# An MLP's seven-product schemes: one PSUM bank for each product, or products chained in shared banks

## The chip, the cores and the metric

The kernel runs on one core of one Trainium2 chip. Its time is the device time of one execution in microseconds (us); for a set of runs the median is given. The core has a matrix engine (PE; its weight loads are shown apart as PEld), three engines for elementwise work (DVE, ACT, POOL), and queues that issue transfers (SP's above all). Matmul results land in PSUM, eight banks of 512 fp32 columns in each of 128 partitions. In this kernel PE, DVE and ACT touch PSUM, and POOL works only in SBUF.

## The reference, cut to what matters

One layer of a flow-matching backbone on 640 tokens (128 of a prompt, 512 of a sample), width 1024: a mixer block, then an MLP with a squared ReLU. The edit touches the MLP alone:

```python
def _ffn_sub(x, shift, scale, gate, w_pre, w_post, w1, w2):
    h = _rms(x, w_pre) * (1 + scale) + shift
    f = jnp.square(jax.nn.relu(h @ w1)) @ w2
    return x + gate * _rms(f, w_post)
```

`w1` is 1024 x 4096 and `w2` 4096 x 1024. All is fp32.

## The kernel before, in words

**Precision.** Every fp32 operand is split into a rounded high part and a remainder (`split`, L165: ACT casts `whi`, then DVE, or POOL where `eng=G`, subtracts to get `wlo`). A product is three matmuls: high x high, high x low, low x high.

**Groups.** The 4096 hidden columns are worked in eight groups of 512, g = 0 to 7. A group has a first product (`ff1`, hidden values from `h` and `w1`), the squared ReLU, and a second product (`ff2`, its share of the output from the hidden values and `w2`). Group 0's first product (`ff1_first`, L1147) is made in the plain way, and so is group 7's second product, after the loop. All others use a scheme that makes a 2 x 2 block product from seven block products instead of eight, with sums of blocks before and after.

**ff1(g), g = 1 to 7 (L1165).** The weight block is cut into A11, A21, A22, A12 and the activations into B11 to B22 (two halves of the width, and the tokens in 64-column halves). POOL makes the weight sums S1 = A21 + A22, S2 = S1 - A11, S3 = A11 - A21, then S2' = A12 - S2, in tiles of `sm` (L1135). Each of the seven products runs in two halves of 12 matmuls with 320 columns, each half in a bank of its own; `ps_ff` (L1143) hands out five banks in turn (two `ps_mm`, three `ps_st`). DVE adds each finished half to a sum in SBUF, in `add` (L1189, recorded at L1191): 7 x 2 = 14 adds, and ACT copies the first product (L1196). `done` (L1186) is the squared ReLU in place, on DVE, four times.

**fops(c) (L1224)** makes ff2's left operands from ff1's four tiles `c11` to `c22`, again sums of blocks on POOL (L1237 to L1243) and splits on ACT and DVE (L1216, L1217).

**ff2(g - 1) (L1256).** The right operands are sums T1, T2, T3, T2' of blocks of `w2`, on POOL. Each of the seven products runs in two halves of 6 matmuls with 512 columns, and each half goes to one of three banks in turn (`ps_t3`, L121: two `ps_tp`, one `ps_tb`). The prompt's tokens have two plain products of 12 matmuls (`prompt`). `collect` (L1250) adds each bank to a running sum in SBUF, on DVE (L1254); for g = 0 it is a copy by ACT (L1252). There are eight such sums, `R[0]` to `R[7]`: one for each product and one for the prompt. What the scheme adds up from its seven products is put off to the end: seven POOL additions of whole sums after the loop (L1326).

**Loop (L1307).** For g = 1 to 7: `ff1(g)`, then `ff2(g - 1)`, then `fops` for g. After it group 7's second product is made, added to the sums (L1347), normalised and stored.

**Order of the work.** The program is built with `schedule_with_timeline_sim=True` (L1445): a planner of the framework orders each engine's instructions from its own estimate of durations, with the written order as priority. So the order in the trace isn't always the written one; PE, for instance, begins the next ff1 between two halves of ff2's last product. Each engine then works through its list in order. Weight loads are issued by SP's queue in order, into five buffers (L1037); a load waits until its buffer's former block has been read for the last time.

Of the kernel before, what the change touches and what calls it, by code (L numbers as in the profile page):

```python
# [18 lines left out]
P = 128  # L19
# [77 lines left out]
def body(ctx: ExitStack, tc: tile.TileContext, I, O, dbg=None):  # L97
# [1037 lines left out]
    def sm(name, a=None, b=None, op=None):  # L1135
        x = fa.tile([P, 1024], F32, tag="sm", name=name, bufs=2)
        if a is not None:
            G.tensor_tensor(x, a, b, op=op)  # L1138
        return x

    ffi = [1]

    def ps_ff():  # L1143
        ffi[0] = (ffi[0] + 1) % 5
        return ps_mm() if ffi[0] < 2 else ps_st(ffi[0] - 2)

    def ff1_first():  # L1147
        c = f_tiles()
        w = {q: load_w(I["w_ff1"][0, i], 4, 256) for q, i in (((0, 0), 0), ((1, 0), 3), ((0, 1), 1), ((1, 1), 2))}
        for t0, t1 in TG:  # L1150
            for fb in range(4):
                wd = (t1 - t0) * 128
                fs = slice(fb % 2 * 128, fb % 2 * 128 + 128)
                ps = ps_ff()
                mm3(by_tile(ps[:, :wd]), [(w[kh, fb // 2][0][:, k, fs], w[kh, fb // 2][1][:, k, fs],
                                           mhi[:, t0:t1, 4 * kh + k], mlo[:, t0:t1, 4 * kh + k])
                                          for kh in range(2) for k in range(4)])
                rl = sm("rl")
                S.activation(rl[:, :wd], ps[:, :wd], AF.Relu)
                for th in range(2):  # L1160
                    r = rl[:, :wd].rearrange("p (t h c) -> p t h c", h=2, c=64)[:, :, th]
                    V.tensor_tensor(c[fb // 2, th][:, fb % 2].rearrange("p (t c) -> p t c", c=64)[:, t0:t1], r, r, op=ALU.mult)
        return c

    def ff1(g):  # L1165
        A11, A21, A22, A12 = [load_raw(I["w_ff1"][g, i]) for i in range(4)]
        c = f_tiles()
        c11, u2, u3, c22 = c[0, 0], c[0, 1], c[1, 0], c[1, 1]

        def prod(raw, B):  # L1170

            hi, lo = split(raw, 4, 256)
            res = []
            for s in range(2):
                fs = slice(s * 128, s * 128 + 128)
                ps = ps_ff()[:, :320]
                for k in range(4):
                    bh, bl = [x[:, k] if len(x.shape) == 3 else x[:, :, k] for x in B]
                    o = ps if len(bh.shape) == 2 else ps.rearrange("p (t c) -> p t c", c=64)
                    PE.matmul(o, hi[:, k, fs], bh, start=(k == 0), stop=False)  # L1180
                    PE.matmul(o, hi[:, k, fs], bl, start=False, stop=False)  # L1181
                    PE.matmul(o, lo[:, k, fs], bh, start=False, stop=(k == 3))  # L1182
                res.append(ps)
            return res

        def done(x):  # L1186
            V.scalar_tensor_tensor(x, x, 0.0, x, op0=ALU.max, op1=ALU.mult)

        def add(out, a, b):  # L1189
            for s in range(2):  # L1190
                V.tensor_tensor(out[:, s], a[:, s], b[s], op=ALU.add)  # L1191

        B11, B12, B21, B22 = [[quad(x, *q) for x in (mhi, mlo)] for q in ((0, 0), (0, 1), (1, 0), (1, 1))]
        p = prod(A11, B11)
        for s in range(2):
            S.copy(u2[:, s], p[s])  # L1196
# [12 lines left out]
        done(u3)  # L1209
        G.tensor_tensor(S2, A12, S2, op=ALU.subtract)  # L1210
        add(u2, u2, prod(S2, B22))
        done(u2)
# [43 lines left out]
    def ff2(g, f):  # L1256
        B11, B21, B12, B22 = [w2_raw(g, *q) for q in ((0, 0), (1, 0), (0, 1), (1, 1))]

        def prod(i, name, w):
            for pair in range(2):  # L1260
                ps = ps_t3()
                mm3(ps, [(f[name][0][:, k, pair * 128 : pair * 128 + 128], f[name][1][:, k, pair * 128 : pair * 128 + 128],
                          w[0][:, k], w[1][:, k]) for k in range(2)])
                collect(R[i][:, pair], ps, g == 0)

        def prompt(n, w0, w1):
            ps = ps_t3()
            mm3(ps, [(f["pr"][0][:, 2 * i + k], f["pr"][1][:, 2 * i + k], w[0][:, k], w[1][:, k])
                     for i, w in enumerate((w0, w1)) for k in range(2)])
            collect(R[7][:, n], ps, g == 0)  # L1270
# [54 lines left out]
    for o, a, b in ((1, 0, 1), (5, 0, 5), (6, 5, 6), (2, 5, 2), (2, 2, 4), (3, 6, 3), (4, 6, 4)):  # L1325
        G.tensor_tensor(R[o], R[a], R[b], op=ALU.add)  # L1326
    with tc.tile_pool(name="fin", bufs=2, side="right", reuse_waits="tile") as fin_:
        gB2 = gate_bcast(1, fin_)
        w = {(kh, nh): split(w2_raw(7, kh, nh), 2, 512) for nh in range(2) for kh in range(2)}
        for blk in (None, (0, 0), (1, 0), (0, 1), (1, 1)):  # L1330
            r = 0 if blk is None else 1
            if blk is None:
                parts = [(slice(0, 128), 0, slice(0, 128))]
                y = [R[7][:, n] for n in range(2)]
                lhs = [[x[:, k] for x in fpr] for k in range(4)]
            else:
                th, pair = blk
                parts = [(slice(64 * j, 64 * j + 64), 1 + 2 * pair + j, slice(64 * th, 64 * th + 64)) for j in range(2)]
                y = [R[1 + 2 * th + n][:, pair] for n in range(2)]
# [119 lines left out]
```

## Time and profile before

| what | value |
|---|---|
| median of 3 runs | 1231.33 us (1230.71 to 1232.45) |
| profiled execution, its own time | 1229.95 us |
| its span, first to last instruction | 1228.0 us |
| mean granted clock of PE | 0.973 |
| loop over g | about 809 to 1196 us |

How to read the rows. A row of the timeline has the start (us), the duration (us), the engine, the source line, the operation, output <- inputs by the program's names, and, in brackets, how long the engine stood idle before it and what ended that. A row of groups has line, engine, operation, output <- inputs, shapes, xcount, then busy time and the mean ns of one, then the idle time before them. A row of stretches has start:end, length, then busy time (and instructions) of PE, PEld, DVE, ACT and POOL, PE's granted clock, the DMA share and GB/s. A row of waits has the waiting engine and line, the releaser, then us in total, times, and the longest. Matmul durations overlap, so the distance between starts is what counts.

### The profile page before, as it was taken

The numbers are of one execution on the slowest core, as the hardware profiler recorded it, in microseconds if no ns is written. First come the engines' busy times: TensorE is split into PE (matmuls) and PEld (weight loads), VectorE is DVE, ScalarE is ACT, GpSimd is POOL, SyncE is SP. The second block draws the span as 40 slices with busy tenths as digits, with TensorE's granted clock in tenths as the row PEclk, the third lists the DMA queues.
The fourth block names the chain that finished last, engine by engine and source line by source line (L and its number), as shares of the span: only waits on it lengthen the run. The fifth ranks groups of instructions, "written<-read, shape, count | busy, mean of one in ns | idle before, by whom it ended". The sixth has DMA issues, their size and how long they took to land. (4 is left out here: it accounts for less than half of the span.)

```text
span 1228.0 us, 24856 instructions
## 1 busy us (share of the span) xinstructions
PE 1123.9 (92%) x10111; PEld 986.2 (80%) x10111; DVE 947.3 (77%) x1689; ACT 478.0 (39%) x910; POOL 494.6 (40%) x322
## 2 busy tenths in 40 slices
PE   5999799898989799988999999989899989898896
PEld 3789799787777688887777899978878879796875
DVE  6568996675677666635756567899999999999996
ACT  5433344252423233224436253445443434344322
POOL 1442416150542110312311406656464556556555
PEclk9999999898989999989999999999999999999999
DMA  9721024444425433645334471021213223121405
GB/s 332 270 95 53 1 93 139 137 129 154 147 68 182 146 110 96 206 152 181 110 103 148 152 275 69 18 87 52 86 52 103 69 69 107 66 86 52 159 31 137
DMA packets 61313, 144.87 MB, mean 118 GB/s; under 512 B 12384, under 2 KB 26000, under 8 KB 61200
## 3 DMA queue, kind: packets, MB, share of 16 engines
q1 hardware_dynamic: 38528, 108.66, 26.2%
q10 hardware_dynamic: 22672, 34.64, 9.0%
q8 instruction: 79, 1.29, 0.4%
q14 instruction: 34, 0.28, 0.1%
HBM read 122.02 MB, written 21.25 MB: 117 GB/s over the span
## 5 line engine op out<-in xcount | busy, mean ns | idle before, releaser
L190 PE MATMUL ps_mm<-hhi,whi 128*128 128x320 f32 x576 | 185.8, 323 | 2.1 <-DVE gbn L244 1.5
L191 PE MATMUL ps_mm<-hlo,whi 128*128 128x320 f32 x576 | 183.1, 318 | 0.0
L192 PE MATMUL ps_mm<-hhi,wlo 128*128 128x320 f32 x576 | 182.8, 317 | 0.1
L171 DVE TENSOR_TENSOR wlo<-raw,whi 128x1024 fp32r<-128x1024 f32 x94 | 153.9, 1647 | 33.7 <-ACT whi L170 33.2
L170 ACT CAST whi<-raw 128x1024 fp32r<-128x1024 f32 x117 | 121.5, 1047 | 114.1 <-PE ps_tp L192 25.4
L190 PEld LDWEIGHTS ps_mm<-hhi,whi 128*128 128x128 f32 x576 | 111.4, 193 | 7.4 <-DVE gbn L244 1.9
L192 PEld LDWEIGHTS ps_mm<-hhi,wlo 128*128 128x128 f32 x576 | 111.4, 193 | 0.6
L191 PEld LDWEIGHTS ps_mm<-hlo,whi 128*128 128x128 f32 x576 | 111.4, 193 | 0.5
L171 POOL TENSOR_TENSOR wlo<-raw,whi 128x1024 fp32r<-128x1024 f32 x23 | 56.7, 2469 | 82.7 <-ACT whi L170 82.4
L1138 POOL TENSOR_TENSOR T<-raw 128x1024 f32<-128x1024 f32 x14 | 37.7, 2692 | 67.9 <-DVE wlo L171 32.6
L171 DVE TENSOR_TENSOR wlo<-T,whi 128x1024 fp32r<-128x1024 f32 x28 | 54.2, 1940 | 0.7 <-ACT whi L170 0.6
L170 ACT CAST whi<-T 128x1024 fp32r<-128x1024 f32 x28 | 29.4, 1053 | 64.0 <-PE ps_st L1181 19.6
L972 POOL TENSOR_SCALAR bias<-bias 128x256 f32<-128x256 f32 x24 | 25.2, 1057 | 70.6 <-DMA bias<-in_bias_dram 70.6
L480 DVE SCALAR_TENSOR_TENSOR y<-cvb,cw,y 128x644 f32<-128x644 f32 x48 | 49.2, 1026 | 0.7
L567 POOL TENSOR_TENSOR W<-cst,ghi 128x512 fp32r<-128x512 f32 x15 | 19.0, 1265 | 71.3 <-PE ps_tp L568 69.2
L1138 POOL TENSOR_TENSOR S<-raw 128x1024 f32<-128x1024 f32 x14 | 34.2, 2441 | 33.5 <-DVE wlo L171 33.5
L1254 DVE TENSOR_TENSOR R<-R,ps_tp 128x512 f32<-128x512 f32 x64 | 42.6, 676 | 2.6 <-PE ps_tp L192 2.3
L1182 PE MATMUL ps_st<-mhi,wlo 128*128 128x320 f32 x128 | 39.2, 309 | 0.3 <-DVE wlo L171 0.3
L1181 PE MATMUL ps_st<-mlo,whi 128*128 128x320 f32 x128 | 39.4, 308 | 0.0
L1180 PE MATMUL ps_st<-mhi,whi 128*128 128x320 f32 x128 | 39.3, 309 | 0.0
L170 ACT CAST whi<-S 128x1024 fp32r<-128x1024 f32 x28 | 29.2, 1047 | 24.8 <-POOL S L1138 24.8
L651 DVE TENSOR_TENSOR tq<-tq,Ud 128x16 f32<-128x16 f32 (+14 forms) x75 | 36.7, 489 | 1.9
(594 smaller groups left out, 3544.8 us busy)
## 6 DMA issues: line engine op xcount, KB each, us to landing
raw<-in_w_ff_dram SPq DMA_DIRECT2D x64, 512.0 KB
raw<-in_w_ada_dram SPq DMA_DIRECT2D x48, 512.0 KB
raw<-in_w_gate_dram SPq DMA_DIRECT2D x16, 512.0 KB
raw<-in_w_dn_dram SPq DMA_DIRECT2D x12, 512.0 KB
gt_d<-gth SPq DMA_DIRECT2D x32, 160.0 KB
gl<-gt_d ACTq DMA_DIRECT2D x16, 320.0 KB
raw<-in_w_qk_dram SPq DMA_DIRECT2D x8, 512.0 KB
raw<-in_w_br_dram SPq DMA_DIRECT2D x8, 512.0 KB
```

The costliest lines, as they stand in the source:

```text
L170: S.copy(hi, raw)
L171: eng.tensor_tensor(lo, raw, hi.bitcast(F32), op=ALU.subtract)
L190: PE.matmul(out, ah, bh, start=(i == 0), stop=False)
L191: PE.matmul(out, ah, bl, start=False, stop=False)
L192: PE.matmul(out, al, bh, start=False, stop=(i == n - 1))
L480: V.scalar_tensor_tensor(y, b[:, j : j + 644], cw[:, mt * 5 + j : mt * 5 + j + 1], y, op0=ALU.mult, op1=ALU.add)
L651: V.tensor_tensor(tq[:, q:, :], tq[:, q:, :], Ud[:, :, q].unsqueeze(1).to_broadcast([P, w, 16]), op=ALU.mult)
L1138: G.tensor_tensor(x, a, b, op=op)
L1180: PE.matmul(o, hi[:, k, fs], bh, start=(k == 0), stop=False)
L1181: PE.matmul(o, hi[:, k, fs], bl, start=False, stop=False)
L1182: PE.matmul(o, lo[:, k, fs], bh, start=False, stop=(k == 3))
L1254: V.tensor_tensor(dst, dst, ps, op=ALU.add)
```

## The change

In both schemes products that a result needs together are now chained in the same PSUM banks: later products add to what is there (`start` is not set for them), and the partial sum is read between two products.

- **ff1** has two bank pairs, `x` (the two `ps_mm`) and `y` (two `ps_st`). On `x` run A11 B11, then S2, S1 and S2' on top of it; on `y` runs A12 B21, and, taken anew, S3 and A22 on top. After A11 B11, S2 and S1, ACT copies the partial sum of `x` into a tile (`so_far`, six copies of half a pair instead of two); DVE adds `y` to a tile three times (six adds of 320 columns instead of 14). The fourth result is read from `x` by two ReLUs and a Square on ACT; the other three squared ReLUs stay on DVE.
- **ff2** chains A11, S2, S1 and S4 on `x` (two `ps_tp`), A12 on a pair `ps_tb` and `ps_st(2)`, and S3 and A22 on the same pair, taken anew. `prompt` uses `ps_tb`. `collect` is called as often as before, but into four sums and one for the prompt. In the first call (g = 0) six of the collects are DVE adds instead of ACT copies, since two products now go into one sum. The order is A11, A12, prompt, S2, S3, S1, A22, S4, prompt instead of A11, A12, prompt, S1, S2, A22, S3, S4, prompt.
- The seven POOL additions after the loop and the tile `R2` are gone, and `sm` has four buffers instead of two. `ff1_first` takes four banks in turn instead of five.

```diff
-        x = fa.tile([P, 1024], F32, tag="sm", name=name, bufs=2)
+        x = fa.tile([P, 1024], F32, tag="sm", name=name, bufs=4)
...
-    def ps_ff():
-        ffi[0] = (ffi[0] + 1) % 5
-        return ps_mm() if ffi[0] < 2 else ps_st(ffi[0] - 2)
+    def ps_ff(i):
+        return ps_mm() if i < 2 else ps_st(i - 2)
...
+        x = [ps_ff(s)[:, :320] for s in range(2)]
+
+        def prod(raw, B, ps, first=True, last=False):
...
+                    PE.matmul(o, hi[:, k, fs], bh, start=(first and k == 0), stop=False, skip_group_check=not first)
...
+        def so_far(out, ps):
             for s in range(2):
-                V.tensor_tensor(out[:, s], a[:, s], b[s], op=ALU.add)
...
-        p = prod(A11, B11)
-        for s in range(2):
-            S.copy(u2[:, s], p[s])
-        add(c11, u2, prod(A12, B21))
-        done(c11)
+                S.copy(out[:, s], ps[s])
+
+        def add(out, ps):
+            for s in range(2):
+                V.tensor_tensor(out[:, s], out[:, s], ps[s], op=ALU.add)
...
+        prod(A11, B11, x)
+        so_far(c[0, 0], x)
+        y = [ps_ff(2 + s)[:, :320] for s in range(2)]
+        prod(A12, B21, y, last=True)
+        add(c[0, 0], y)
+        done(c[0, 0])
         S1 = sm("S1", A21, A22, ALU.add)
         S2 = sm("S2", S1, A11, ALU.subtract)
-        add(u2, u2, prod(S2, TT[1]))
-        p = prod(S1, TT[0])
+        prod(S2, TT[1], x, False)
+        so_far(c[1, 0], x)
         S3 = sm("S3", A11, A21, ALU.subtract)
-        add(u3, u2, prod(S3, TT[2]))
-        add(u2, u2, p)
-        add(c22, u3, p)
-        done(c22)
-        add(u3, u3, prod(A22, B12))
-        done(u3)
+        y = [ps_ff(2 + s)[:, :320] for s in range(2)]
+        prod(S3, TT[2], y)
+        prod(S1, TT[0], x, False)
+        so_far(c[1, 1], x)
+        add(c[1, 1], y)
+        done(c[1, 1])
         G.tensor_tensor(S2, A12, S2, op=ALU.subtract)
-        add(u2, u2, prod(S2, B22))
-        done(u2)
+        prod(S2, B22, x, False, True)
+        for s in range(2):
+            S.activation(c[0, 1][:, s], x[s], AF.Relu)
+        S.activation(c[0, 1], c[0, 1], AF.Square)
+        prod(A22, B12, y, False, True)
+        add(c[1, 0], y)
+        done(c[1, 0])
...
+        x = [ps_tp() for _ in range(2)]
+
+        def banks():
+            return [ps_tb(), ps_st(2)]
+
+        def prod(name, w, ps, dst, first=True, last=False, new=False):
...
+                collect(R[dst][:, pair], ps[pair], new and g == 0)
...
-            ps = ps_t3()
+            ps = ps_tb()
...
         b11 = split(B11, 2, 512)
-        prod(0, "A11", b11)
+        prod("A11", b11, x, 0, new=True)
         b21 = split(B21, 2, 512)
-        prod(1, "A12", b21)
+        prod("A12", b21, banks(), 0, last=True)
         prompt(0, b11, b21)
         T1 = sm("T1", B12, B11, ALU.subtract)
-        prod(4, "S1", split(T1, 2, 512))
         T2 = sm("T2", B22, T1, ALU.subtract)
-        prod(5, "S2", split(T2, 2, 512))
+        prod("S2", split(T2, 2, 512), x, 2, False, new=True)
+        T3 = sm("T3", B22, B12, ALU.subtract)
+        y = banks()
+        prod("S3", split(T3, 2, 512), y, 3, new=True)
+        prod("S1", split(T1, 2, 512), x, 3, False)
         G.tensor_tensor(T2, B21, T2, op=ALU.subtract)
-        prod(3, "A22", split(T2, 2, 512))
-        T3 = sm("T3", B22, B12, ALU.subtract)
-        prod(6, "S3", split(T3, 2, 512))
+        prod("A22", split(T2, 2, 512), y, 2, False, True)
         b22 = split(B22, 2, 512)
-        prod(2, "S4", b22)
+        prod("S4", b22, x, 1, False, True, new=True)
         prompt(1, split(B12, 2, 512, eng=G), b22)
...
-            R2 = fa.tile([P, 3, 2, 512], F32, tag="R2", name="R2")
-            R = [R[:, i] for i in range(5)] + [R2[:, i] for i in range(3)]
+            R = [R[:, i] for i in range(5)]
...
-    for o, a, b in ((1, 0, 1), (5, 0, 5), (6, 5, 6), (2, 5, 2), (2, 2, 4), (3, 6, 3), (4, 6, 4)):
-        G.tensor_tensor(R[o], R[a], R[b], op=ALU.add)
```

More of the change, by code (lines that the diff above doesn't have):

```diff
@@ L1186, in done @@
-        def done(x):
-            V.scalar_tensor_tensor(x, x, 0.0, x, op0=ALU.max, op1=ALU.mult)
-        def add(out, a, b):
-            for s in range(2):
-                V.tensor_tensor(out[:, s], a[:, s], b[s], op=ALU.add)
-        B11, B12, B21, B22 = [[quad(x, *q) for x in (mhi, mlo)] for q in ((0, 0), (0, 1), (1, 0), (1, 1))]
-        p = prod(A11, B11)
-        for s in range(2):
-            S.copy(u2[:, s], p[s])
-        add(c11, u2, prod(A12, B21))
-        done(c11)
+                    bh, bl = [t[:, k] if len(t.shape) == 3 else t[:, :, k] for t in B]
@@ L1333, in body @@
                 parts = [(slice(0, 128), 0, slice(0, 128))]
-                y = [R[7][:, n] for n in range(2)]
+                y = [R[4][:, n] for n in range(2)]
                 lhs = [[x[:, k] for x in fpr] for k in range(4)]
```

34 lines of the change are left out of this document (14 added, 20 removed).

## The prediction

> **What bounds the kernel now.** I read the page's totals first, then busy time by stretches, then who waits for whom inside the MLP loop (809 to 1196 us), the only place the edit touches.
>
> ```profile
> span 1228.0 us, 24856 instructions
> PE 1123.9 (92%) x10111; PEld 986.2 (80%) x10111; DVE 947.3 (77%) x1689; ACT 478.0 (39%) x910; POOL 494.6 (40%) x322
> ```
>
> Over the whole span PE looks like the limit. One turn of the loop reads otherwise. Two starts of the same POOL operation (S2 = A12 - S2, L1210), four turns apart, give the turn: (1135.93 - 917.62)/4 = 54.6 us.
>
> ```profile
> 917.62 2.40 POOL L1210 TENSOR_TENSOR S<-raw,S 128x1024 f32<-128x1024 f32 x1 [3.57 <-DVE wlo L171]
> 1135.93 2.40 POOL L1210 TENSOR_TENSOR S<-raw,S 128x1024 f32<-128x1024 f32 x1 [3.57 <-DVE wlo L171]
> ...
> 1026.60:1081.20 54.60, 50.64 (x280) 44.63 (x278) 53.80 (x60) 21.23 (x29) 30.72 (x13) 1.00 0.23 78
> ...
> PE ps_tp L190 <- DVE R L1254: 8.5, 7, 1.9
> PE ps_tb L190 <- DVE R L1254: 6.4, 5, 1.9
> ```
>
> In the stretch of one turn (busy PE, PEld, DVE, ACT, POOL) DVE works 53.8 of 54.6 us and PE 50.6. The waits over four turns say why PE stands still: 14.9 us, 3.7 a turn, all in the second product (ff2), each time for a DVE add into R that must empty a PSUM bank. So DVE sets the turn and PE is close behind. How close, the starts of matmuls in an unbroken stream tell:
>
> ```profile
> 920.30 0.31 PE L1180 MATMUL ps_st<-T2h,whi 128*128 128x320 f32 x1
> 923.83 0.31 PE L1180 MATMUL ps_st<-T0h,whi 128*128 128x320 f32 x1
> ...
> 907.75 0.39 PE L190 MATMUL ps_tp<-whi,S4h 128*128 128x512 f32 x1
> 908.88 0.39 PE L192 MATMUL ps_tp<-whi,S4l 128*128 128x512 f32 x1
> ```
>
> 24 matmuls of 320 columns lie between the first two: 3.53/24 = 0.147 us each; five steps of 512 columns take 1.13: 0.227 each. A turn has 7 x 24 = 168 of the first kind and 7 x 12 + 24 = 108 of the second: 24.7 + 24.5 = 49.2 us. The edit changes neither count, so no turn gets below 49.2: at most 5.4 us can be won per turn.
>
> Not all of DVE's 53.8 us is its own work:
>
> ```profile
> L171 DVE TENSOR_TENSOR wlo<-raw,whi 128x1024 fp32r<-128x1024 f32 x30 | 59.1, 1970 | 0.0
> L171 DVE TENSOR_TENSOR wlo<-S,whi 128x1024 fp32r<-128x1024 f32 x20 | 24.3, 1216 | 0.2
> L1191 DVE TENSOR_TENSOR c<-c,ps_st 128x320 f32<-128x320 f32 x42 | 19.3, 480 | 0.2
> L1191 DVE TENSOR_TENSOR c<-c,ps_mm 128x320 f32<-128x320 f32 x28 | 13.0, 480 | 0.1
> ```
>
> The same subtraction takes 1.22 us in one group and 1.97 in another; adds that read PSUM always take 0.48. The timeline shows what lengthens the first kind, and what runs beside the second:
>
> ```profile
> 895.80 2.40 POOL L1138 TENSOR_TENSOR S<-raw 128x1024 f32<-128x1024 f32 x1 [3.72 <-DVE wlo L171]
> ...
> 896.08 3.20 DVE L171 TENSOR_TENSOR wlo<-T,whi 128x1024 fp32r<-128x1024 f32 x1
> ...
> 921.84 0.87 DVE L1191 TENSOR_TENSOR c<-c,ps_mm 128x320 f32<-128x320 f32 x2
> ...
> 921.99 2.39 POOL L1138 TENSOR_TENSOR S<-raw 128x1024 f32<-128x1024 f32 x1 [1.97 <-DVE wlo L171]
> ...
> 924.99 0.48 DVE L1191 TENSOR_TENSOR c<-c,ps_st 128x320 f32<-128x320 f32 x1
> ...
> 931.73 3.27 POOL L1138 TENSOR_TENSOR T<-raw,T 128x1024 f32<-128x1024 f32 x1
> ...
> 932.66 0.47 DVE L1191 TENSOR_TENSOR c<-c,ps_mm 128x320 f32<-128x320 f32 x1
> 933.17 1.28 DVE L1191 TENSOR_TENSOR c<-c,ps_st 128x320 f32<-128x320 f32 x3
> 934.49 0.89 DVE L1191 TENSOR_TENSOR c<-c,ps_mm 128x320 f32<-128x320 f32 x2
> ...
> 940.35 0.48 DVE L1191 TENSOR_TENSOR c<-c,ps_mm 128x320 f32<-128x320 f32 x1
> ...
> 940.58 2.39 POOL L1138 TENSOR_TENSOR T<-raw 128x1024 f32<-128x1024 f32 x1 [5.58 <-DVE wlo L171]
> ...
> 941.35 2.71 DVE L171 TENSOR_TENSOR wlo<-T,whi 128x1024 fp32r<-128x1024 f32 x1
> 943.98 0.81 DVE L1187 SCALAR_TENSOR_TENSOR c<-c 128x640 f32<-128x640 f32 x1
> 944.72 0.67 DVE L1254 TENSOR_TENSOR R<-R,ps_tb 128x512 f32<-128x512 f32 x1
> ...
> 945.45 0.50 PE L190 MATMUL ps_tb<-whi,prh 128*128 128x512 f32 x1 [1.84 <-DVE R L1254]
> ...
> 946.89 0.63 PE L192 MATMUL ps_tb<-whi,prl 128*128 128x512 f32 x1
> ...
> 947.50 1.27 DVE L1254 TENSOR_TENSOR R<-R,ps_tp 128x512 f32<-128x512 f32 x2
> ```
>
> POOL runs from 895.80 to 898.20; the DVE subtraction that started at 896.08 ends at 899.28, one plain duration after POOL. So DVE operations with two inputs in SBUF stand still while POOL works; the adds from PSUM do not. Of a turn's 14 adds, 8 (921.84, 932.66 to 934.49) run while POOL holds a following subtraction back anyway; 6 (the first at 924.99, the last at 940.35) run while POOL is idle.
>
> **The change, part by part.**
>
> *ff1, adds.* 14 adds become 6, so 8 go. Back to back they start 0.40 apart ((1.28 - 0.48)/2), with a gap between them 0.51 (932.66 to 933.17): 0.43 each, 3.4 us. The fourth squared ReLU (L1187) goes to ACT: 0.74 from start to next start (943.98 to 944.72). Upper bound of the gain per turn: 4.2 us. Lower bound: adds under a POOL operation are worth nothing, since the next subtraction then waits for POOL; by proportion 8 x 6/14 = 3.4 lie free, 1.5 us, and with the 0.74 that is 2.2. I take 2.3, near the lower end, because after the edit even fewer operations are left that can run beside POOL. Seven ff1 calls: **-16.1** (bounds -15.4 and -29.4).
>
> *ff1, work that arrives on ACT.* Four more copies out of PSUM, two ReLUs of the same shape, and one Square of 640 columns:
>
> ```profile
> L1196 ACT COPY c<-ps_st 128x320 f32<-128x320 f32 x7 | 2.8, 429 | 10.9 <-PE ps_mm L1182 6.1 <-DVE prl L1217 4.8
> L1351 ACT ACTIVATE fsq<-R 128x512 f32<-128x512 f32 x10 | 6.3, 630 | 16.4 <-DVE R L1347 15.9 <-DVE fs L1356 0.5
> L170 ACT CAST whi<-raw 128x1024 fp32r<-128x1024 f32 x53 | 55.7, 1050 | 64.9 <-PE ps_tp L192 25.4 <-PE ps_tb L192 19.4 <-PE ps_st L1181 12.5
> ```
>
> 6 x 0.43 + 0.74 (between 0.63 for 512 and 1.05 for 1024) = 3.3 us on an engine busy 21.2 of 54.6. Its idle time hides it, so 0; without that cover 3.3 x 7 = 23. The moved squared ReLU is longer there (2 x 0.43 + 0.74 = 1.6 us against 0.74), but DVE is full and ACT 39% busy. The Trainium skill speaks against this step: "ScalarE: Activation LUTs", Rules for kernel authors, wants relu and products on VectorE. By that rule it would stay on DVE, and the sum would lose 0.74 x 7 = 5.2 us of its gain.
>
> *ff1, new waits of PE.* S2's product writes onto bank pair x after the copies of x; the 24 matmuls of A12 B21 cover that (3.5 us against 0.86). S2' follows S1's product in the same pair directly; the cover is the pair's other half, 12 x 0.147 = 1.76 us, against a copy 0.43 behind at most one cast 1.05: fits, with 0.3 to spare. S3 onto y waits for DVE's adds with 3.5 us of cover; a subtraction stretched to 3.2 in front leaves about 0.5 short. Behind that wait stand all later products, and ACT's casts that wait for PE to free weights. I take 0, the upper bound is 1 us a turn, 7 in all. The two extra buffers for POOL's sums remove waits such as the 5.58 above; POOL is idle 24 us a turn, so 0. A22's split and hence the load of B22, which needs its buffer on SP's queue, come one product (3.5 us) later, and T2 is used one product earlier; T2's split ended at 944.06 (941.35 + 2.71) and would be needed at about 945.45 + 12 x 0.227 = 948.2: 4.1 us of slack, so 0.
>
> *ff2.* Seven products, 14 adds into R and two for the prompt stay: 0. In its first call (g = 0) six copies by ACT become DVE adds, 0.60 each, 3.6 us, part of it beside POOL: **+2.7** (0 to 3.6). Now three banks go round, so a product's half has two halves of cover, 2 x 6 x 0.227 = 2.7 us, before its bank must be empty. In the new order most halves have three (4.1 us), S3 two, and the prompt's first product one (1.4 us). Longer cover moves PE's waits but takes nothing off DVE, so 0 while DVE sets the turn; the prompt's product is rival B.
>
> *After the loop.* Seven POOL sums disappear:
>
> ```profile
> L1326 POOL TENSOR_TENSOR R<-R,R 128x1024 f32<-128x1024 f32 x4 | 10.6, 2650 | 0.1
> L1326 POOL TENSOR_TENSOR R<-R 128x1024 f32<-128x1024 f32 x3 | 8.9, 2973 | 7.9 <-DVE R L1254 7.8
> ...
> 1166.25 0.79 PE L190 MATMUL ps_tp<-whi,prh 128*128 128x512 f32 x1 [4.38 <-DVE R L1254]
> ...
> 1166.25:1171.53 5.28, 5.28 (x12) 4.13 (x13) 5.28 (x10) 1.05 (x1) 1.25 (x1) 0.50 0.26 91
> 1171.53:1189.76 18.23, 17.29 (x73) 13.40 (x72) 15.64 (x17) 6.31 (x6) 9.38 (x5) 0.99 0.08 30
> ```
>
> 19.5 us of POOL, but from 1171.53 PE runs nearly unbroken (17.29 of 18.23) and DVE is not full. What they can have cost is PE's idle 0.94 there plus about half as much again later: **-1.4**. The 4.38 us wait at 1161.9 with the 12 matmuls after it at clock 0.50 (5.28 us instead of 2.73) is worth up to 6.9 more if DVE arrives there earlier; lower bound 0, and I take 0 because the prompt's product, which waits there, is the one whose cover shrinks.
>
> Sum: -16.1 + 2.7 - 1.4 = -14.8. The profiled execution took 1229.95 us (span 1228.0), so 1215.2; the median of the runs, 1231.33, lies 1.4 above it: **1216.5 us**.
>
> **The rivals.**
>
> *A: DVE's whole saving counts.* Adds move out from under POOL as the order changes, 4.2 x 7 = 29.4; DVE is earlier at 1161.9 and the 6.9 come too: -29.4 + 2.7 - 1.4 - 6.9 = -35, 1196 us. For it: PE's floor of 49.2 allows it. Against: DVE and PE would then both be full, with four banks between them.
>
> *B: PSUM cover is lost, slower.* The prompt's product now writes the single tb bank right after A12's first half, so it waits for the third add into R, not the second. In the rows above the second starts at 944.72 and the third at 947.50: PE's wait of 1.84 becomes 4.6. A wait of 4.38 has shown clock 0.50 behind it, and that cost 2.55 us. PE's turn would be 49.2 + 4.6 + 2.55 = 56.4 us, more than DVE's, 1.8 over the turn of now: 7 x 1.8 = +12.6, less the 1.4 of the tail: 1242 us. It decides once PE's waits and clock losses are over 5.4 us a turn (54.6 - 49.2). Against: DVE arrives there 2 to 4 us earlier after a lighter ff1, the other waits of ff2 get longer cover, and the planner may put S2's product ahead of the prompt's. Behind the wait of 1.84, too, the matmul at 946.89 took 0.63 instead of 0.39, as those at clock 0.50 do, though this stretch is one of few. The Trainium skill's "TensorE: Matmul & The Clock Gate" (The HAM clock gate) lets the clock fall to half after an idle window of about 3.4 us; by it a wait of 1.84 us would be free and one of 4.6 us would not, so on the shorter wait the trace is stricter than the page.
>
> *C: no change.* The removed adds turn into waits for POOL and for banks y, and the 0.5 us shortfalls eat the rest: 1229 to 1233. For it: 8 of 14 adds already run under POOL. Against: 6 do not.
>
> **How the numbers follow.** Forecast (1205 to 1225) 0.52, A 0.20, C 0.11, B 0.17. The range runs from just above A's 1196 into B: 1197 to 1238; the forecast's own range is 1205 to 1225. A difference under 0.2% (2.5 us) can't be told from none. Faster: 0.52 + 0.20 + 0.02 of C = 0.74; within: 0.09; slower: 0.17.
>
> **What would show it.** Turn length between two starts of POOL's S2 = A12 - S2: 52.3 if right, 50.4 for A, over 54.6 for B. DVE adds of 320 columns 42 instead of 98 in all, DVE's busy share per turn still over 95%. The prompt's product: a wait under 2 us; over 4 with clock 0.50 behind it is B. ACT about 24.5 us busy a turn; new PE waits on ACT copies (ff1) near 0. It is wrong if PE waits in ff1, if POOL operations cover more of DVE's subtractions than now, or if the loop's gain is not where the difference lies.

## The result and the profile after

The changed kernel takes 1278.0 us (median of 4 runs, 1277.22 to 1285.36) against 1231.38: a ratio of 1.040 (95% interval 1.037 to 1.043). It is slower by 47 us, outside the predicted range, and by a way that no rival named.

The totals of the page, changed kernel:

```profile
span 1275.6 us, 24839 instructions
PE 1126.3 (88%) x10111; PEld 995.4 (78%) x10111; DVE 937.1 (73%) x1632; ACT 496.5 (39%) x953; POOL 473.0 (37%) x315
```

DVE has 10 us less of busy time than before, ACT 18 more, POOL 22 less: the work moved the way that was announced. The span grew by 47.6 all the same. The five turns between the second and the seventh start of S2' = A12 - S2, as one stretch (length, then busy PE, PEld, DVE, ACT, POOL, clock, DMA share, GB/s), kernel before:

```profile
863.29:1135.93 272.64, 251.75 (x1361) 220.78 (x1361) 268.43 (x295) 106.16 (x141) 153.47 (x65) 0.99 0.23 78
```

and the changed kernel, with one of its turns below:

```profile
863.59:1182.19 318.60, 259.95 (x1374) 233.62 (x1374) 270.37 (x249) 122.03 (x177) 153.76 (x67) 0.92 0.20 67
1054.60:1118.20 63.60, 51.76 (x275) 46.45 (x275) 54.07 (x51) 24.26 (x36) 30.82 (x14) 0.92 0.21 67
```

318.60 - 272.64 = 46.0 of the 47.6 us lie in these five turns: 63.7 us each instead of 54.5. DVE's busy time per turn did not fall (54.1 against 53.7), and it is no longer full: it now stands idle for 9.6 us a turn. The waits of PE over the five turns name the place (us in total, times, longest), changed kernel:

```profile
PE ps_mm L1177 <- ACT c L1183: 46.7, 5, 9.7
PE ps_tp L1274 <- DVE wlo L171: 5.7, 5, 1.3
PE ps_st L1273 <- DVE R L1259: 5.0, 4, 1.3
```

Once a turn PE waits 9.3 us (46.7/5) in ff1, with S2's product on bank pair `x`, for ACT's copy of the first partial sum. ACT, in its turn, waits for DVE (groups of the whole kernel, changed; over the five turns alone the second one went from 1216 ns before to 2024):

```profile
L1183 ACT COPY c<-ps_mm 128x320 f32<-128x320 f32 x42 | 17.1, 424 | 58.9 <-DVE S2l L1222 31.7 <-PE ps_mm L1179 24.0 <-DVE S4l L1222 3.2
L171 DVE TENSOR_TENSOR wlo<-S,whi 128x1024 fp32r<-128x1024 f32 x28 | 56.3, 2029 | 2.0 <-ACT whi L170 2.0
```

The copy takes 0.42 us but waits for S2l, a subtraction by DVE that belongs to fops. These subtractions of fops (L1222) are what grew: 76.9 us over the five turns instead of 53.6, or 4.7 us a turn, about what the adds and the ReLU took away; those of the weights (L171) fell from 123.0 to 119.5 in sum. The timeline of that place, changed kernel:

```profile
1045.52 1.29 POOL L1242 TENSOR_TENSOR c<-c,c 128x512 f32<-128x512 f32 x1 [4.27 <-DVE A22l L1222]
1048.29 2.40 POOL L1138 TENSOR_TENSOR T<-raw 128x1024 f32<-128x1024 f32 x1 [1.48 <-DMA raw<-in_w_ff_dram]
1050.65 1.75 POOL L1244 TENSOR_TENSOR c<-c,c 128x512 f32<-128x512 f32 x1
1052.48 2.16 POOL L1246 TENSOR_TENSOR c<-c,c 128x512 f32<-128x512 f32 x1
1054.60 2.40 POOL L1210 TENSOR_TENSOR S<-raw,S 128x1024 f32<-128x1024 f32 x1
1056.95 1.32 POOL L1248 TENSOR_TENSOR c<-c,c 128x512 f32<-128x512 f32 x1
1060.65 3.03 POOL L1138 TENSOR_TENSOR T<-raw,T 128x1024 f32<-128x1024 f32 x1 [2.39 <-DMA raw<-in_w_ff_dram]
...
1054.00 4.62 DVE L1222 TENSOR_TENSOR prl<-c,prh 128x128 fp32r<-128x128 f32 x4
1058.54 0.68 DVE L1222 TENSOR_TENSOR S3l<-c,S3h 128x512 fp32r<-128x512 f32 x1
1059.14 2.35 DVE L171 TENSOR_TENSOR wlo<-S,whi 128x1024 fp32r<-128x1024 f32 x2
1061.41 2.82 DVE L1222 TENSOR_TENSOR S2l<-c,S2h 128x512 fp32r<-128x512 f32 x1
...
1054.86 0.61 ACT L1221 CAST S2h<-c 128x512 fp32r<-128x512 f32 x1
...
1064.27 0.75 ACT L1183 COPY c<-ps_mm 128x320 f32<-128x320 f32 x2 [5.35 <-DVE S2l L1222]
...
1064.74 0.63 PE L1177 MATMUL ps_mm<-T2h,whi 128*128 128x320 f32 x1 [9.44 <-ACT c L1183]
```

Read it from below. The first copy of ff1(g+1) goes into the single buffer `c11`, that is `c[0,0]`. fops of group g had made S2, an operand of ff2, in that same tile in place, and S2l is its late reader. S2l ends at 1064.23 (1061.41 + 2.82), 8.9 us after PE has run out of work at 1055.30 (1064.74 - 9.44). Now from above: T1's sum (`T<-raw`) and S2' (L1210) stand between POOL's four sums of fops (L1242 to L1248), which take from 1045.52 to 1058.27, 12.8 us; and T2's sum (1060.65 to 1063.68) lies beside S2l, which takes 2.82 us instead of 0.68. But POOL is not what S2l waits for last: S2's sum ended at 1054.64 (1052.48 + 2.16), ACT's cast S2h at 1055.47, and S2l began only at 1061.41. In these 5.9 us DVE went through its own list, prl, S3l and two `wlo<-S`, prl lengthened beside POOL's S2' and fourth sum (4.62 us against 2.70 in the kernel before). So most of the 8.9 us lies in the order and the lengthening of DVE's list. The same place in the kernel before, the first and last of the four sums, S2l and the first copy:

```profile
1015.95 1.30 POOL L1237 TENSOR_TENSOR c<-c,c 128x512 f32<-128x512 f32 x1 [1.47 <-DVE A22l L1217]
...
1021.81 1.62 POOL L1243 TENSOR_TENSOR c<-c,c 128x512 f32<-128x512 f32 x1
...
1024.49 0.68 DVE L1217 TENSOR_TENSOR S2l<-c,S2h 128x512 fp32r<-128x512 f32 x1
...
1029.82 0.43 ACT L1196 COPY c<-ps_mm 128x320 f32<-128x320 f32 x1 [3.04 <-DVE prl L1217]
```

There the four sums stood together (7.5 us), S2l was not stretched and stood ahead of prl, and the copy, into another tile, waited for another subtraction of DVE (prl); no wait of PE followed, with five banks going round.

The same turn by stretches, changed kernel:

```profile
1055.30:1064.74 9.44, 0.01 (x1) 0.00 (x0) 9.44 (x8) 2.31 (x5) 7.05 (x4) 0.70 0.17 56
1064.74:1067.60 2.86, 2.85 (x11) 2.86 (x12) 2.86 (x2) 0.28 (x1) 1.72 (x1) 0.50 0.00 0
1067.60:1084.00 16.40, 16.40 (x106) 16.23 (x106) 8.03 (x11) 5.33 (x9) 0.00 (x0) 0.95 0.20 65
```

First DVE is full and PE does nothing; then PE runs for 2.9 us at a clock of 0.50; then PE is full for 16.4 us, DVE is half idle and POOL does nothing. Two engines that ran side by side now wait for each other in turn.

### The profile page after: what moved, and what is told of

The parts are those of the page before. It is cut to its first block, busy times and chain, and to the rows that moved or that the text cites. A ratio compares the mean times of both kernels' runs of the same rounds, so it can differ in the third digit from the quotient of the medians.

```text
span 1275.6 us, 24839 instructions
## 1 busy us (share of the span) xinstructions
PE 1126.3 (88%) x10111; PEld 995.4 (78%) x10111; DVE 937.1 (73%) x1632; ACT 496.5 (39%) x953; POOL 473.0 (37%) x315
## 4 chain that ended last, share of the span: by engine, by line
PE 53%; DVE 25%; DMA 5%; issue 4%; ACT 2%; POOL 0%; ACTq 0%; DVEq 0%; SPq 0%
PE ps_mm L190 7%; DVE wlo L171 7%; PE ps_mm L191 7%; PE ps_mm L192 7%; PE ps_mm L1177 2%; PE ps_mm L1178 2%; PE ps_mm L1179 2%; DVE R L1259 2%; DVE tq L651 2%; DVE S2l L1222 1%; DVE Yd L652 1%; PE ps_st L1177 1%; DVE y L480 1%; PE ps_st L1178 1%; PE ps_st L1179 1%
## 5 line engine op out<-in xcount | busy, mean ns | idle before, releaser
L171 DVE TENSOR_TENSOR wlo<-raw,whi 128x1024 fp32r<-128x1024 f32 x94 | 136.2, 1459 | 66.4 <-ACT whi L170 65.3
L171 POOL TENSOR_TENSOR wlo<-raw,whi 128x1024 fp32r<-128x1024 f32 x23 | 60.3, 2624 | 86.0 <-ACT whi L170 85.7
L1177 PE MATMUL ps_mm<-T2h,whi 128*128 128x320 f32 x56 | 24.7, 440 | 64.5 <-ACT c L1183 64.5
L1177 PEld LDWEIGHTS ps_mm<-T2h,whi 128*128 128x128 f32 x56 | 16.1, 288 | 66.3 <-ACT c L1183 66.3
L1296 POOL TENSOR_TENSOR T<-raw,T 128x1024 f32<-128x1024 f32 x7 | 16.9, 2407 | 128.8 <-DVE wlo L171 128.8
L171 DVE TENSOR_TENSOR wlo<-S,whi 128x1024 fp32r<-128x1024 f32 x28 | 56.3, 2029 | 2.0 <-ACT whi L170 2.0
L171 DVE TENSOR_TENSOR wlo<-T,whi 128x1024 fp32r<-128x1024 f32 x28 | 41.2, 1492 | 19.1 <-ACT whi L170 19.1
L1138 POOL TENSOR_TENSOR S<-raw 128x1024 f32<-128x1024 f32 x14 | 39.8, 2845 | 27.4 <-DMA raw<-in_w_ff_dram 14.4
L480 DVE SCALAR_TENSOR_TENSOR y<-cvb,cw,y 128x644 f32<-128x644 f32 x48 | 49.2, 1024 | 0.7
L1183 ACT COPY c<-ps_mm 128x320 f32<-128x320 f32 x42 | 17.1, 424 | 58.9 <-DVE S2l L1222 31.7
```

The lines of the kernel that those rows point to most:

```text
L171: eng.tensor_tensor(lo, raw, hi.bitcast(F32), op=ALU.subtract)
L480: V.scalar_tensor_tensor(y, b[:, j : j + 644], cw[:, mt * 5 + j : mt * 5 + j + 1], y, op0=ALU.mult, op1=ALU.add)
L1177: PE.matmul(o, hi[:, k, fs], bh, start=(first and k == 0), stop=False, skip_group_check=not first)
```

## The experiments

All are timed beside the kernel before on the same chip (medians 1231.0, 1230.7 and 1229.5 us in the three sets); ratios have 95% intervals. A turn is the mean of five, measured like above. The letters of the theories are explained where they appear in an expectation; W is the reading above: the copy waits for its tile's old reader.

**one_spare.** A second buffer for the tile of the first copy:

```diff
-        return {q: fa.tile([P, 2, 320], F32, tag=n, name=n) for q, n in QN.items()}
+        return {q: fa.tile([P, 2, 320], F32, tag=n, name=n, bufs=2 if n == "c11" else 1) for q, n in QN.items()}
```

> The changed kernel, with a second buffer for the tile c11 alone, which takes the first partial sum of ff1. Theory W (the first partial sum is copied into the tile whose old content, the operand S2 of ff2, is read last by DVE's split S2l; until then bank pair x is blocked and PE waits 9.25 us a turn, with the clock at half behind it): the wait before the T2h matmuls falls under 1 us, but the second partial sum goes into the tile that S4l reads last, so part of the wait, 4 to 6 us, comes back before S1's product; turn 57 to 60 us instead of 63.7, time 1240 to 1258. Rival P (DVE is late as a whole, whatever tile is written): turn stays over 62, time 1270 to 1280. Rival F (ff2's chained banks set the turn): no change either, 1275 to 1281.

1266.5 us, ratio 1.027 (1.023 to 1.032), turn 60.2. Only a quarter of the loss goes, and the time lies outside the intervals of W, P and F alike. Now PE waits for DVE's adds and for later copies instead (from 860 us to 1157 us of this kernel):

```profile
PE ps_st L1177 <- DVE c L1187: 17.6, 9, 3.0
PE ps_mm L1177 <- ACT c L1183: 12.4, 5, 4.6
```

**other_tiles.** No memory added: in every second group the tiles of `c[0,0]` and `c[1,1]`, and of `c[1,0]` and `c[0,1]`, change places, so the first copy meets another old reader.

```diff
+        fcnt[0] += 1
+        tag = {q: QN[q if fcnt[0] % 2 else OLD[q]] for q in QN}
+        return {q: fa.tile([P, 2, 320], F32, tag=tag[q], name="c") for q in QN}
```

> The changed kernel; the four tiles of ff1 change places in every second group, so that the first partial sum goes into the tile that held S1 (free as soon as POOL has made S2 from it), the second into that of S3, the third into that of S2, the last into that of S4. No memory is added and no operation. W: PE's wait before the T2h matmuls falls from 9.25 to at most 3 us a turn, with no half clock behind it in most turns; turn 52 to 56 us, time 1212 to 1235. Rival P: the copies wait for DVE all the same, turn over 60, time over 1255. Rival F: 1275 to 1281.

1245.9 us, 1.011 (1.008 to 1.015), turn 57.8: 32 of the 47 us go, less than W expected (at most 1235 us). All four buffers are still there, and so is the order of the work on POOL and DVE:

```profile
1035.10 2.40 POOL L1143 TENSOR_TENSOR T<-raw 128x1024 f32<-128x1024 f32 x1 [1.48 <-DMA raw<-in_w_ff_dram]
...
1048.22 2.86 DVE L1227 TENSOR_TENSOR S2l<-c,S2h 128x512 fp32r<-128x512 f32 x1
...
1045.46 0.75 ACT L1188 COPY c<-ps_mm 128x320 f32<-128x320 f32 x2 [3.18 <-DVE prl L1227]
...
PE ps_mm L1182 <- ACT c L1188: 17.8, 5, 3.8
```

T1's sum stands second among POOL's sums, and S2l is as late, but the copy no longer waits for it: it goes as soon as prl has read its tile. PE's wait for the copies falls to 3.6 us a turn (17.8/5).

**two_spares.** `c11` and `c21` with two buffers each, and `sm` with three, since four don't fit beside them.

```diff
-        return {q: fa.tile([P, 2, 320], F32, tag=n, name=n) for q, n in QN.items()}
+        return {q: fa.tile([P, 2, 320], F32, tag=n, name=n, bufs=2 if n in ('c11', 'c21') else 1) for q, n in QN.items()}
...
-        x = fa.tile([P, 1024], F32, tag="sm", name=name, bufs=4)
+        x = fa.tile([P, 1024], F32, tag="sm", name=name, bufs=3)
```

> The changed kernel with second buffers for the two tiles that take the first and the second partial sum (c11 and c21), and three buffers instead of four for POOL's sums, so that it fits. W: no copy waits for the old content any more; PE's wait before the T2h matmuls under 1 us; turn 51 to 54, time 1205 to 1225. If DVE's shorter list decides (rival A of the prediction) it is the lower end, with POOL holding DVE's subtractions back the upper. Rival P: over 1255. Rival F: 1275 to 1281.

1238.3 us, 1.006 (1.003 to 1.009), turn 56.8. Of the 47 us 39 are back (7.3 over its own kernel before), but it is still slower than before, which W had not said. And two things were changed at once, so the credit can't be given to the tiles; three_sm, below, settles that. PE no longer waits for a copy here. Its largest wait is now that of S3's product for DVE's adds of `y`, 2.1 us a turn (10.4/5):

```profile
PE ps_st L1177 <- DVE c L1187: 10.4, 5, 2.9
```

**ff2_alone.** ff1 as before, ff2 and the four `sm` buffers as in the change.

```diff
-        x = [ps_ff(s)[:, :320] for s in range(2)]
-        prod(A11, B11, x)
-        so_far(c[0, 0], x)
...
+        c11, u2, u3, c22 = c[0, 0], c[0, 1], c[1, 0], c[1, 1]
+        p = prod(A11, B11)
+        for s in range(2):
+            S.copy(u2[:, s], p[s])
```

(against the changed kernel)

> ff1 as before (five banks in turn, 14 adds, one copied product) and ff2 as in the changed kernel (chained banks, four sums, no sums after the loop). W: the loss is in ff1, so this is at the kernel before, 1226 to 1236 (the sum of the prediction for this part is +2.7 - 1.4). Rival F: ff2's banks carry the loss, 1255 to 1280.

1262.6 us, 1.025 (1.020 to 1.030), turn 60.0. ff1's chaining isn't needed for most of the loss; F was right here, W wrong. The order at the place above is that of the changed kernel (T1's sum second on POOL, prl, S3l and two splits ahead of S2l on DVE). With five banks and the old target the first copy doesn't wait for S2l, but PE waits in ff1 for DVE's adds and ACT's copies, 28.8 us over the five turns (14.7 in ff2_three_sm, below). What stays the same in this kernel and in the changed one: ff2's order, its chained banks, and the fourth buffer.

**old_order_swapped.** The kernel before with the order of two products exchanged.

```diff
         T1 = sm("T1", B12, B11, ALU.subtract)
-        prod(4, "S1", split(T1, 2, 512))
         T2 = sm("T2", B22, T1, ALU.subtract)
         prod(5, "S2", split(T2, 2, 512))
+        prod(4, "S1", split(T1, 2, 512))
```

> The kernel before, with one exchange: in ff2 the product S2 comes ahead of S1 (POOL's order of sums stays T1, T2, T2', T3). Nothing is added or removed. Theory O (the new order of ff2 is the second cause: POOL's sums then run beside DVE's two-input SBUF work instead of beside its reads of PSUM): POOL time beside DVE reads of PSUM falls from 10.7 us a turn towards 7, the turn is 56 to 59 us, 1240 to 1260 us. Rival K (the chaining or the four buffers is the cause, not the order): overlap stays at 10 to 11, turn 54.5, 1228 to 1235 us.

1228.4 us, 0.999 (0.996 to 1.002), turn 54.5. This exchange costs nothing that can be measured. (It is a part of the new order; S3 ahead of S1 wasn't tried alone.)

**old_tile_wait.** The kernel before with the tiles of `c[0,0]` and `c[0,1]` exchanged in every second group, so that its first copy, too, goes where S2l reads.

```diff
+    OLD = {(0, 0): (0, 1), (0, 1): (0, 0), (1, 0): (1, 0), (1, 1): (1, 1)}
...
+        tag = {q: QN[q if fcnt[0] % 2 else OLD[q]] for q in QN}
```

> The kernel before with the tiles of c[0,0] and c[0,1] exchanged in every second group, so that ff1's first copy goes into the tile that DVE reads last for S2l. No work is added. Theory W: the copy stands for that read here too; five banks go round, so PE has one half more (1.8 us) than in the changed kernel before it must wait: 5 to 8 us of PE wait a turn in ff1, turn 59 to 63, 1255 to 1290 us. Rival (the wait only hurts because two bank pairs are left): no PE wait over 2 us, 1229 to 1238 us.

1228.5 us, 0.998 (0.995 to 1.001). No wait. The timeline of this kernel says why:

```profile
1027.40 0.68 DVE L1222 TENSOR_TENSOR S2l<-c,S2h 128x512 fp32r<-128x512 f32 x1
...
1032.54 0.43 ACT L1201 COPY c<-ps_mm 128x320 f32<-128x320 f32 x1 [2.84 <-DVE prl L1222]
```

S2l ends at 1028.08, 4.5 us ahead of the copy. So the shared tile alone is no loss; S2l must also be late. That theory, W as first put, falls. The time is the rival's, but as the copy never waited for S2l, the run doesn't test whether five banks would have covered such a wait. It leads to Q: what makes S2l late is the fourth `sm` buffer.

**three_sm.** The changed kernel with one figure changed:

```diff
-        x = fa.tile([P, 1024], F32, tag="sm", name=name, bufs=4)
+        x = fa.tile([P, 1024], F32, tag="sm", name=name, bufs=3)
```

> The changed kernel with three sm buffers instead of four; its tiles stay single. Theory Q (the fourth buffer lets the planner put POOL's sum T1 between the sums of fops, which makes S2l late, and only then does the first copy have to stand for its tile): the copy's wait, 9.4 us a turn in the changed kernel, falls under 3, turn 57 to 59 us, 1235 to 1252 us. Theory W alone (the single tile is enough by itself): the wait stays at 7 to 9 us, turn 62 to 64, 1262 to 1280 us.

1241.1 us, 1.011 (1.008 to 1.014), turn 57.5. One buffer less gives 35 of the 47 us back (11.7 over its own kernel before). Its timeline at the same place:

```profile
1027.68 2.22 POOL L1242 TENSOR_TENSOR c<-c,c 128x512 f32<-128x512 f32 x1 [3.56 <-DVE A22l L1222]
1029.97 1.29 POOL L1244 TENSOR_TENSOR c<-c,c 128x512 f32<-128x512 f32 x1
1031.34 1.63 POOL L1246 TENSOR_TENSOR c<-c,c 128x512 f32<-128x512 f32 x1
1033.05 1.62 POOL L1248 TENSOR_TENSOR c<-c,c 128x512 f32<-128x512 f32 x1
1035.84 2.35 POOL L1210 TENSOR_TENSOR S<-raw,S 128x1024 f32<-128x1024 f32 x1 [1.16 <-DVE wlo L171]
1040.76 3.90 POOL L1138 TENSOR_TENSOR T<-raw 128x1024 f32<-128x1024 f32 x1 [2.57 <-DVE wlo L171]
...
1036.28 2.46 DVE L1222 TENSOR_TENSOR S2l<-c,S2h 128x512 fp32r<-128x512 f32 x1
...
1038.97 0.75 ACT L1183 COPY c<-ps_mm 128x320 f32<-128x320 f32 x2 [2.13 <-DVE prl L1222]
...
1039.45 0.63 PE L1177 MATMUL ps_mm<-T2h,whi 128*128 128x320 f32 x1 [3.64 <-ACT c L1183]
```

The four sums of fops are together again (1027.68 to 1034.67, 7.0 us), T1 comes after them, S2l ends 2.9 us after PE ran dry (1038.74 against 1039.45 - 3.64 = 1035.81) instead of 8.9, and the wait is 3.6 us instead of 9.4. DVE's list has changed too: prl, on which the copy waits now, stands behind S2l. Q's interval for the wait, under 3 us, is missed by a little; the time is inside. Its waits over five turns, and the stretch of a wait with the one after it:

```profile
PE ps_mm L1177 <- ACT c L1183: 17.4, 5, 3.7
```

```profile
977.94:981.58 3.64, 0.00 (x1) 0.00 (x0) 3.64 (x6) 1.51 (x4) 2.35 (x1) 0.80 0.12 16
981.58:984.50 2.92, 2.92 (x11) 2.92 (x12) 2.92 (x5) 1.22 (x2) 1.61 (x1) 0.50 0.45 160
```

**ff2_three_sm.** ff2_alone with three buffers.

```diff
-        x = fa.tile([P, 1024], F32, tag="sm", name=name, bufs=4)
+        x = fa.tile([P, 1024], F32, tag="sm", name=name, bufs=3)
```

> ff2_alone (ff1 of before, ff2 of after) with three sm buffers instead of four. Theory Q: the sums of fops stand together on POOL again, turn 55 to 57 us instead of 60.0, 1232 to 1246 us. Rival F (ff2's chaining or its order carries the loss, not the buffer): 59 to 60.5 us, 1253 to 1268 us.

1230.9 us, 1.001 (0.999 to 1.004), turn 55.7. 30 us of ff2_alone's loss of 31.6 are the fourth buffer. ff2's chaining and order, with it taken away, cost nothing that can be measured in the whole, though two parts cancel in it: the turn is 1.2 us longer than before, and what follows the last mark is 6.3 us shorter (1229.6 - 1143.9 = 85.7 against 1228.0 - 1135.9 = 92.1). F falls.

**ff1_alone.** The kernel before with the new ff1, S1's product put ahead of S3's so that two `sm` buffers do, and the tiles exchanged as in other_tiles.

```diff
+        prod(S1, TT[0], x, False)
+        so_far(c[1, 1], x)
         S3 = sm("S3", A11, A21, ALU.subtract)
         y = [ps_ff(2 + s)[:, :320] for s in range(2)]
         prod(S3, TT[2], y)
-        prod(S1, TT[0], x, False)
-        so_far(c[1, 1], x)
```

(against the changed ff1)

> The kernel before with the new ff1 alone, S1's product ahead of S3's so that two sm buffers do, and the tiles exchanged in every second group as in other_tiles; ff2, its eight sums and the seven additions at the end are as before. Theory O: DVE's own work is 4.2 us a turn less and the overlap with POOL stays near 9, so a turn of 51 to 53 us, 1207 to 1225 us. Rival K2 (what DVE no longer does comes back as waiting for POOL, whatever ff2 does): DVE still busy 53 to 54 a turn, overlap 7, turn 54 to 55.5, 1227 to 1240 us.

1236.3 us, 1.004 (1.002 to 1.007), turn 56.4. Neither theory: the time is K2's, by another way. The five turns of this kernel, and what PE waits for in them:

```profile
856.84:1138.98 282.14, 259.78 (x1371) 224.95 (x1370) 243.12 (x250) 119.69 (x176) 144.65 (x65) 0.98 0.24 75
```

```profile
PE ps_tp L190 <- DVE R L1262: 8.8, 9, 2.0
PE ps_mm L1180 <- ACT c L1186: 7.4, 9, 2.2
PE ps_tb L190 <- DVE R L1262: 3.9, 4, 1.9
PE ps_st L1180 <- ACT whi L170: 1.6, 4, 0.4
```

Here DVE did become lighter, 48.6 us a turn against 53.7, and the turn grew by 1.9 us. PE's waits for DVE in ff2 fell from 3.8 to (8.8 + 3.9)/5 = 2.5 us a turn, but 1.5 us of waits for the copies came (7.4/5), in part by my own order: S1's product follows S2's on the same pair, with the copy between. The rest, 56.4 - 49.2 - 4.3 = 2.9 us a turn, was 1.1 in the kernel before (54.5 - 49.2 - 4.2): part of it is a lower clock (0.98 against 0.99 over the five turns), and what else it is stays open.

**fewer_sums.** two_spares with the raw blocks A21 and B22 in the place of POOL's sums S3 and T3. These two sums are left out.

```diff
-        S3 = sm("S3", A11, A21, ALU.subtract)
+        S3 = A21
...
-        T3 = sm("T3", B22, B12, ALU.subtract)
+        T3 = B22
```

> The kernel two_spares without POOL's sums S3 and T3: the raw blocks A21 and B22 stand in for them, so 2 of POOL's 13 operations a turn (about 5.3 us) are left out, and results change. Theory P (DVE's work on two SBUF inputs and POOL's work shut each other out, and together they set the turn): DVE's waits for POOL fall by about 4 us, the turn from 56.8 to 52 to 54, 1203 to 1220 us. Rival (POOL's work costs nothing, PE's waits and DVE's own work set the turn): 1233 to 1241 us.

1212.3 us, 0.984 (0.979 to 0.989), turn 53.3 against 56.8. Five turns of two_spares and of this kernel:

```profile
864.37:1148.47 284.10, 257.75 (x1386) 227.78 (x1385) 267.10 (x250) 119.64 (x178) 153.43 (x66) 0.98 0.23 75
```

```profile
859.94:1126.25 266.31, 253.24 (x1382) 225.01 (x1381) 251.29 (x250) 121.00 (x178) 130.06 (x55) 0.99 0.25 80
```

POOL works (153.43 - 130.06)/5 = 4.7 us less a turn, DVE is 3.2 us less busy though its list of operations is the same, and the turn is 3.6 us shorter. POOL, busy 54% of the turn, is on the path. That it is so by way of DVE's standing still fits the 3.2 us; that two products no longer wait for a sum of POOL may have a part in it, and wasn't tried apart.

**old_b12_dve.** The kernel before, with one remainder made on DVE instead of POOL.

```diff
-        prompt(1, split(B12, 2, 512, eng=G), b22)
+        prompt(1, split(B12, 2, 512), b22)
```

> The kernel before with the remainder of block B12 (2.37 us a turn on POOL) made on DVE (1.13 us). Theory P (POOL's time and DVE's two-input work add up): 1.2 us less in all, turn 53.6 to 54.4 us, 1223 to 1230 us. Rival (DVE's own work alone sets the turn): 55.3 to 55.8, 1236 to 1241 us.

1229.8 us, 1.000 (0.998 to 1.002). The rival is out. The time is just inside P's interval, but P as a plain sum of the two engines' times is not shown: in the profiled execution the turn is 55.1 us, not 53.6 to 54.4.

**old_relu_act.** The kernel before with the squared ReLU on ACT:

```diff
         def done(x):
-            V.scalar_tensor_tensor(x, x, 0.0, x, op0=ALU.max, op1=ALU.mult)
+            S.activation(x, x, AF.Relu)
+            S.activation(x, x, AF.Square)
```

> The kernel before with one part of the change: the squared ReLU of ff1, four times a turn on DVE, becomes a Relu and a Square of 640 columns on ACT. DVE has 4 x 0.74 = 3.0 us less of the work that POOL shuts out, ACT 4 x 1.5 = 5.9 more (21 to 27 a turn). Theory P: turn 52.3 to 53.6 us, 1217 to 1227 us. Rival (the way through ACT is longer and the sums of fops start later, so DVE's splits wait): 54.5 to 56, 1231 to 1243 us.

1221.3 us, ratio 0.9955 (0.993 to 0.998): a little faster than both kernels, with nothing of the chaining. Its five turns:

```profile
860.81:1128.37 267.56, 254.12 (x1361) 223.14 (x1361) 247.48 (x275) 132.03 (x181) 151.27 (x66) 0.98 0.24 79
```

53.5 us a turn instead of 54.5. DVE is 4.2 us lighter (49.5 against 53.7), for 3.0 us of operations taken away. A quarter of DVE's relief reaches the turn; why not more, no run shows. The Trainium skill's "ScalarE: Activation LUTs" (Rules for kernel authors) wants relu and products on VectorE because that engine is quicker at them; it is quicker here too (0.74 us against two operations of 0.74 on ACT), but the kernel gains by the slower engine, as that one is idle for half of the turn.

## Why the prediction was wrong, point by point

**"The two extra buffers for POOL's sums remove waits ...; POOL is idle 24 us a turn, so 0."** This step failed, together with the next one. The fourth buffer costs 35 us (the changed kernel against three_sm, each over its own kernel before) and, with ff1 as before, 30 (ff2_alone against ff2_three_sm). The step looked at what POOL would no longer wait for, not at what would then stand in front of what: the planner moved T1's sum, for which there was now room, and S2' between the sums of fops, and those carry DVE's splits. A wait that had kept a list in a good order was taken for a loss. What the runs show is the price of the buffer and that the order goes with it: in the turns read of the changed kernel, one_spare, other_tiles and ff2_alone, all with four, T1's sum stands second among POOL's sums and prl ahead of S2l on DVE; in three_sm, two_spares and ff2_three_sm the four sums stand together and prl behind S2l. Which of the two lists carries the loss I did not try apart; in the changed kernel S2h was ready 5.9 us before S2l began, so DVE's list has the larger part there.

**"S2's product writes onto bank pair x after the copies of x; the 24 matmuls of A12 B21 cover that (3.5 us against 0.86). ... I take 0, the upper bound is 1 us a turn."** Failed: 9.3 us a turn, and the clock behind it. The cover was compared with how long the copy takes, not with when it may begin. A copy has a target as well as a source, and the target's old content had a reader late in DVE's list. Before, the first copy went to `u2` = `c[0,1]` and waited for a reader too, but five banks went round; now the bank pair hangs on that one tile. With three buffers 3.5 us a turn of this wait stay (17.4/5), and the spare tiles of two_spares bring 4.3 us in time (11.7 to 7.3), which the overlapping intervals of the two ratios hardly tell from none. With four buffers the tile weighs far more: other_tiles moves the copy's target alone and 32 us go. The same paragraph's 0.5 us for S3, with 1 us as the upper bound for all the new waits, was too little as well: 2.1 us a turn in two_spares.

**"ff1, adds: -16.1 (bounds -15.4 and -29.4)."** The work did go: 42 adds instead of 98, as said. In ff1_alone DVE is 5.1 us a turn lighter, 2.8 more than I took. But the turn did not follow: PE's waits stayed at 4.3 us a turn (4.2 before), 1.5 of them now for copies, which the prediction held to be 0, and its unassigned rest grew from 1.1 to 2.9. In two_spares it did not even reach DVE's busy time. With the rows of POOL's and DVE's timelines laid side by side over the five turns, per turn, before and in two_spares: DVE's reads of PSUM fell from 16.7 us to 13.2, POOL's 30.7 us ran beside them for 6.1 us instead of 10.7, and so POOL ran beside DVE's operations on SBUF for 23.9 us instead of 20.4. These grew from 39.4 to 42.0 us, with 0.74 us less to do. That is rival C's sentence, the removed adds turn into waits for POOL, and the lower bound of -2.2 a turn did not allow for it. It is no rule: in ff1_alone, with the same reads gone, POOL ran beside the SBUF operations for only 17.0 us. The Trainium skill's "SBUF — State Buffer" (Who interferes with whom) has a DVE instruction with two SBUF inputs and a GpSimd instruction that reads SBUF shut each other out for the whole instruction; S2l's 2.82 us beside a POOL sum agrees with it.

**"ff1, work that arrives on ACT: 0."** Right: ACT is busy 24.4 us a turn, 24.5 was said, and in old_relu_act 5.2 us more than before (132.03 against 106.16 over five turns) cost nothing either.

**"ff2: +2.7" and "after the loop: -1.4".** The first turn, with g = 0, is 1.8 us longer than before (863.59 - 808.11 = 55.5 between its marks against 53.7), against 2.7 - 2.3 = 0.4 by the prediction's terms; what lies after the last mark is 1.3 us longer, not 1.4 shorter. Both are small in the changed kernel, and neither was tried alone. ff2_three_sm holds both terms: +1.4 us in all, not told from none, against +1.3 by the sum. That is luck, since its turn is 1.2 us longer, where the prediction had 0, and its end 6.3 us shorter.

**Rival B, the prompt's product on one bank.** It did not come: no wait for `ps_tb` stands among PE's waits of the five turns. Its mechanism, a long wait of PE with half the clock behind it, came at another place. The prediction's last sentence named the signs, PE waiting in ff1 and POOL covering more of DVE's subtractions, and both appeared (POOL beside DVE's SBUF operations for 24.6 us a turn in the changed kernel, 20.4 before); no chance was given to them.

So the 47 us come from the fourth buffer and the copy's tile together, and how they are shared out depends on which is taken away first. Time over the kernel before:

| | the copy's old tile | tiles exchanged or doubled |
|---|---|---|
| four buffers | +46.6 (changed kernel) | +14.9 (other_tiles) |
| three buffers | +11.7 (three_sm) | +7.3 (two_spares) |

The buffer makes DVE's subtractions late, and the tile makes that delay into a wait of PE: either remedy alone takes 32 to 35 us away. What is left, some 5 to 8, the new ff1 costs where there is no fourth buffer (ff1_alone +5.6, two_spares +7.3). Why the new ff1 gains nothing, although DVE is lighter, is only partly known: DVE is held up by POOL in two_spares, and in ff1_alone part of PE's longer turn is unassigned.

## What to carry to other kernels

Ask of every new copy when its target is free, not only how long it takes: follow the tile back to the last reader of what it held. More buffers are an edit to the order of the work: where a planner sets the order, look which operations may now come earlier and what they will stand in front of. Where DVE and POOL shut each other out, an idle share of POOL is no room, and taking work off DVE counts by what the next engine then lets through: here about a third of 3.0 us.

## What the runs showed of the hardware

DVE's reads of PSUM don't stand still beside POOL: 0.48 us an add in both kernels, while `wlo<-S`, with two inputs in SBUF, went from 1.22 to 2.02 us over the five turns (the subtractions from `raw` and `T` became shorter, 1.97 to 1.68 and 1.98 to 1.47: which ones lie beside POOL changed). In two_spares POOL's work came to lie on the other operations when such reads were removed; in ff1_alone it did not. After waits of 9.4 and of 3.6 us PE ran at clock 0.50 for about 2.9 us; the Trainium skill's "TensorE: Matmul & The Clock Gate" (The HAM clock gate), which sets an idle window of about 3.4 us, agrees with both. Behind the wait of 1.84 us in the kernel before the clock was 0.50 too (946.50 to 949.80), which that window alone does not explain.
